# Latent attention with the values stationary and two heads in one product's columns, and filler pieces placed in other spots

## The chip, the cores and the metric

The kernel runs on one core of a Trainium2 chip. The metric is the device time of one execution in microseconds (us), median of the runs. The core has five engines that run side by side and wait for one another by semaphores: TensorE (PE in the rows; its weight loads are PEld), VectorE (DVE), ScalarE (ACT), GpSimd (POOL) and SyncE (SP, which only issues transfers here). Each engine works through its instructions in the order in which the program lists them.

## The reference, cut to what matters

A first block mixes four branches over 1024 tokens of width 1024, then a feed-forward part and a gate; a second block has linear attention of two kinds and 16 experts. The change touches the latent attention and the state-space branch (SSD) of the first block, the start of its feed-forward part, and the gated linear attention of the second block.

```python
def mla_mixer(c_q, c_kv, k_r, cos, sin, q_norm, w_uq, kv_norm, w_ukv):   # 8 heads, 64 + 32 wide
    ...
    for blk in range(s // Q_BLOCK):                                        # 8 blocks of 128 queries
        q0, kend = blk * Q_BLOCK, (blk + 1) * Q_BLOCK
        sc = (jnp.einsum('bqhd,bkhd->bhqk', q_nope[:, q0:kend], k_nope[:, :kend])
              + jnp.einsum('bqhd,bkd->bhqk', q_rope[:, q0:kend], k_rope[:, :kend]))
        ...
        sc = jnp.where(ki <= qi, sc, -jnp.inf)
        pr = jax.nn.softmax(sc, axis=-1).astype(v.dtype)
        outs.append(jnp.einsum('bhqk,bkhd->bqhd', pr, v[:, :kend]))

def ssd_mixer(z, xbc, dt, conv_w, conv_b, dt_bias, a_log, d_skip, norm_g): # 8 chunks of 128 tokens
    ...
    lmat = jnp.exp(segsum(a))
    cb = jnp.einsum('bclgn,bcsgn->bgcls', cm, bm)
    y_diag = jnp.einsum('bgrcls,bcsgrp->bclgrp', cb[:, :, None] * lmat, xdt)
```

## The kernel before, in words

All large products are made of three products each (helper `mm3`, lines 104 to 106): an operand is split into a high part and a low part (helper `split`, lines 94 and 96: ACT writes the high part, DVE the low one), and hi x hi, hi x lo and lo x hi are summed in PSUM. Their tiles are called `mm`. Operands of plain float32 are multiplied directly; the trace then has two weight loads and two matmuls for one product, called two passes here.

A queue of generators holds such work that nothing waits for at once: the `gates` products of the first block (16 weight chunks, 4 units each, a unit in three pieces of 9, 9 and 6 matmuls of 512 columns), then the first parts of the branch merge (`merge_ahead`, `merge_ahead0`), in the second block the `projections`. `fill(n)` takes n pieces from the queue and places them at that point of the program. The framework then orders the instructions of each engine by its own estimate, near the order of the program.

**SSD** (lines 409 to 480). For each of 8 chunks: `fill(6)`; transposes of the input (`s_tp`); `s_cb`; then for two groups g: POOL writes `s_al` (line 436), PE makes `s_sg` from it (line 440), ACT takes the exponential into `s_m` (line 442), DVE multiplies `s_m` by a mask (line 443), and PE makes `s_yd` of it (line 446, four heads of 64 columns); then `s_yo` and `s_ct` (lines 451, 456).

**Latent attention** (`mla`). Four head groups hg of two heads each. In each group: keys and values (`kv_tile`), queries (`q_tile`), turned by PE (`m_kt`, line 583); then 16 steps s = (i, h) over 8 query blocks i and 2 heads h. A step has the scores `sc` of 128 queries against n = 128(i+1) keys (line 604; PSUM tile `sc` exists once), the maximum on DVE (lines 607, 608), the exponential and its sum on ACT (line 611), the transposes of the weights by 128 columns (`m_pt`, line 629), copied to SBUF by DVE or ACT (`m_pT`, lines 632, 634), and the product with the values `m_o` (line 638): the weights' transpose is stationary (128 x 128), 64 columns of values `m_v` stream. DVE divides by the sum (`m_ot`, lines 640, 641). After both heads PE transposes the result (`m_yt`, line 644), ACT copies it and POOL issues its store. `scores` of the next step stand ahead of the transposes of this one, and `fill(1 + s % 2)` between transposes and `m_o`.

**Feed-forward start** (group g == 0): tokens 512 to 1023 are normed (`norm_half`), then eight products `ff1`. **Gated linear attention** (`gla`): four steps of `decays` (DVE and ACT) and `states` (transposes `g_ktp` line 1305, products `g_ct` line 1312), `fill(2)` between; then scores `g_s` (line 1361), where two heads use 64 rows of the array each.

## Time and profile before

| what | before |
|---|---|
| median of 3 runs | 3830.4 us (3830.1 to 3832.64) |
| profiled execution, its own time | 3829.97 us |
| its span, first to last instruction | 3828.3 us |
| PE busy | 3645.7 us, 95% of the span |
| DVE, ACT, POOL busy | 57%, 42%, 16% |
| mean granted clock of TensorE | 0.98 of full speed |

The profile is one execution recorded by the hardware. A busy PE is not PE at its peak, since matmuls are pipelined: how long a run of them really takes is read from the distance of the starts. A granted clock of 1.00 is the level of 2.4 GHz, and a mean below it says that a part of the stretch ran at 1.2 GHz.

### The profile page before, as it was taken

The page shows a single profiled execution, that of the slowest core. Times are in us where ns is not written, and L with a number is a line of the kernel's source. Part 1 is how long each engine was busy: PE and PEld are TensorE (multiplying, and loading weights), DVE is VectorE, ACT ScalarE, POOL GpSimd, SP SyncE. Part 2 cuts the span into 40 slices and gives each one's busy share as a digit, 9 for nine tenths or more (in the row PEclk, how much of TensorE's full clock was granted, in tenths as well). Part 3 has the DMA queues.
Part 4 walks back from the last instruction along what each step waited for, and adds up shares of the span by engine and source line. Part 5 has one row for each costly group of instructions (what it writes and reads, how often), then busy time and mean ns, then how long its engine had stood idle before and what let it go on. Part 6 is the DMA issues. An engine that isn't in the chain of part 4 may idle for free.

```text
span 3828.3 us, 50597 instructions
## 1 busy us (share of the span) xinstructions
PE 3645.7 (95%) x19648; PEld 3023.6 (79%) x19648; DVE 2184.7 (57%) x3304; ACT 1595.1 (42%) x2310; POOL 618.8 (16%) x731
## 2 busy tenths in 40 slices
PE   8999899999999899999999999989996999999997
PEld 6787688888779888888888988878985677777775
DVE  5425523333455566555435556575554688877777
ACT  7432243333333222222224656445242566654555
POOL 0002310101122200000000211222331222222111
PEclk9999999999999999999999999999997999999999
DMA  4211111221366423332213252223366799998987
GB/s 124 74 51 53 63 51 57 68 65 51 121 196 184 132 79 93 110 96 92 88 45 105 78 144 65 78 79 113 115 219 237 248 354 364 370 347 325 356 335 267
DMA packets 309037, 583.07 MB, mean 152 GB/s; under 512 B 27342, under 2 KB 211756, under 8 KB 308796
## 3 DMA queue, kind: packets, MB, share of 16 engines
q1 hardware_dynamic: 286508, 509.52, 39.0%
q0 software_dynamic: 22288, 70.31, 5.4%
q8 instruction: 155, 2.54, 0.3%
q14 instruction: 86, 0.70, 0.1%
HBM read 513.66 MB, written 66.09 MB: 151 GB/s over the span
## 4 chain that ended last, share of the span: by engine, by line
PE 68%; DVE 5%; issue 4%; ACT 3%; DMA 3%; POOL 2%; SPq 0%; DVEq 0%; POOLq 0%; ACTq 0%
PE mm L104 13%; PE mm L105 13%; PE mm L106 13%; PE mm L1831 5%; PE mm L1828 5%; PE mm L1829 5%; PE mm L1827 5%; PE sc L604 2%; PE m_o L638 1%; DMA w_raw<-in_w_in_dram 1%; DVE w_lo L96 1%; PE m_pt L629 1%; DMA m_g<-gates 1%; DVE e_lo L1804 1%; PE g_s L1361 1%
## 5 line engine op out<-in xcount | busy, mean ns | idle before, releaser
L104 PE MATMUL mm<-hh_hi,w_hi 128*128 128x512 f32 x1872 | 748.7, 400 | 5.4 <-ACT p_u L321 2.1
L105 PE MATMUL mm<-hh_lo,w_hi 128*128 128x512 f32 x1872 | 738.0, 394 | 0.1
L106 PE MATMUL mm<-hh_hi,w_lo 128*128 128x512 f32 x1872 | 737.1, 394 | 0.5 <-DVE w_lo L96 0.5
L1804 DVE TENSOR_TENSOR e_lo<-e_raw,e_hi 128x1408 fp32r<-128x1408 f32 (+1 forms) x308 | 502.5, 1671 | 59.2 <-ACT e_hi L1803 57.5
L96 DVE TENSOR_TENSOR w_lo<-w_raw,w_hi 128x1024 fp32r<-128x1024 f32 (+4 forms) x284 | 348.9, 1244 | 245.9 <-ACT w_hi L94 244.3
L1803 ACT ACTIVATE e_hi<-e_raw 128x1408 fp32r<-128x1408 f32 (+1 forms) x308 | 408.7, 1373 | 139.7 <-PE mm L1829 67.4
L104 PEld LDWEIGHTS mm<-hh_hi,w_hi 128*128 128x128 f32 x1872 | 354.0, 189 | 81.4 <-issue 5.1
L106 PEld LDWEIGHTS mm<-hh_hi,w_lo 128*128 128x128 f32 x1872 | 353.5, 189 | 77.6 <-issue 2.7
L105 PEld LDWEIGHTS mm<-hh_lo,w_hi 128*128 128x128 f32 x1872 | 354.3, 189 | 71.6 <-issue 3.3
L94 ACT ACTIVATE w_hi<-w_raw 128x1024 fp32r<-128x1024 f32 (+4 forms) x284 | 273.6, 985 | 326.8 <-PE mm L105 177.7
L104 PE MATMUL mm<-w_hi,hh_hi 128*128 128x256 f32 x1152 | 334.4, 291 | 0.0
L105 PE MATMUL mm<-w_lo,hh_hi 128*128 128x256 f32 x1152 | 328.5, 285 | 0.0
L106 PE MATMUL mm<-w_hi,hh_lo 128*128 128x256 f32 x1152 | 327.4, 285 | 0.0
L104 PEld LDWEIGHTS mm<-w_hi,hh_hi 128*128 128x128 f32 x1152 | 221.6, 193 | 4.1 <-issue 0.2
L105 PEld LDWEIGHTS mm<-w_lo,hh_hi 128*128 128x128 f32 x1152 | 222.0, 193 | 2.0 <-issue 1.5
L106 PEld LDWEIGHTS mm<-w_hi,hh_lo 128*128 128x128 f32 x1152 | 221.6, 193 | 0.1
L1827 PE MATMUL mm<-e_hi,e_xh 128*128 128x512 f32 x540 | 208.0, 409 | 0.0
L1828 PE MATMUL mm<-e_lo,e_xh 128*128 128x512 f32 x540 | 203.8, 377 | 0.0
L1829 PE MATMUL mm<-e_hi,e_xl 128*128 128x512 f32 x540 | 203.6, 377 | 0.0
L105 PE MATMUL mm<-w_lo,a_hi 128*128 128x512 f32 x512 | 199.6, 390 | 0.0
L104 PE MATMUL mm<-w_hi,a_hi 128*128 128x512 f32 x512 | 199.6, 390 | 0.0
L106 PE MATMUL mm<-w_hi,a_lo 128*128 128x512 f32 x512 | 199.3, 389 | 0.0
(653 smaller groups left out, 6625.4 us busy)
## 6 DMA issues: line engine op xcount, KB each, us to landing
e_raw<-in_w_exp_down_dram SPq DMA_DIRECT2D x112, 768.0 KB
e_raw<-in_w_exp_gate_dram SPq DMA_DIRECT2D x90, 704.0 KB
e_raw<-in_w_exp_up_dram SPq DMA_DIRECT2D x90, 704.0 KB
w_raw<-in_w_in_dram SPq DMA_DIRECT2D x82, 512.0 KB
w_raw<-in_w_ff_dram SPq DMA_DIRECT2D x64, 512.0 KB
w_raw<-in_w_ada_dram SPq DMA_DIRECT2D x48, 512.0 KB
e_nat<-in_w_exp_up_dram SPq DMA_DIRECT2D x32, 704.0 KB
e_nat<-in_w_exp_gate_dram SPq DMA_DIRECT2D x30, 704.0 KB
```

The costliest lines, as they stand in the source:

```text
L94: S.activation(hi, src, AF.Copy, scale=1.0 if scale is None else scale)
L96: V.tensor_sub(lo, src, hi.bitcast(F32))
L104: P.matmul(ps, ah, bh, start=start and k == 0, stop=False)
L105: P.matmul(ps, ah, bl, start=False, stop=False)
L106: P.matmul(ps, al, bh, start=False, stop=stop and k == nk - 1)
L604: P.matmul(sc[:, b:e], qT[:, h, i * 128:n], kT[:, h, b:e], start=True, stop=e < n)
L1803: S.activation(hi[:, :n], r[:, :n], AF.Copy)
L1804: V.tensor_sub(lo[:, :n], r[:, :n], hi[:, :n].bitcast(F32))
L1827: P.matmul(ps, x[0][:, k], w[0][:, c0:c1], start=k == 0, stop=False)
L1828: P.matmul(ps, x[0][:, k], w[1][:, c0:c1], start=False, stop=False)
L1829: P.matmul(ps, x[1][:, k], w[0][:, c0:c1], start=False, stop=k == last)
L1831: P.matmul(ps, x[2](k), w[:, c0:c1], start=k == 0, stop=k == last)
```

## The change

In SSD the six pieces of filler of a chunk stand in three places: one ahead of the chunk, three between the two groups' `s_sg`, two between the two groups' `s_yd`; both groups' `s_m` are started before the first `s_yd`. In the attention the weights are divided by their sum on DVE before they are transposed (n columns, not 64), the values become the stationary operand (128 x 64) and 128 columns of transposed weights stream; the two heads write to partitions 0 to 63 and 64 to 127 of the same `m_o` tile, so the result is feature-major and `m_yt` on PE and `m_ot` on DVE fall away. For i of 4 and more, the first 512 keys and the rest are two separate groups of products. Buffers: `m_pT` 2 to 3, `m_kx` 3 to 2, `m_yt` 2 to 1. The filler's amount in SSD and attention stays the same (6 pieces a chunk, 3 pieces a query block). In the feed-forward start the norm of each 128 tokens follows one product. In `gla` the first of four steps has `fill(4)`.

```diff
@@ -406,7 +406,7 @@
             ssq = sp.tile([128, NT], F32, name="s_ssq")
             B8 = lambda t: t[:, :, None].to_broadcast([128, 8, 64])
             for c in range(NT):
-                fill(6)
+                fill(1)
                 tk = slice(c * 128, (c + 1) * 128)
                 p = ps_ax("s_tp")
                 for ft in range(4):
@@ -430,8 +430,8 @@
                     P.transpose(p[:, :128], xT[:, 4, tk], ident)
                     bt = sp.tile([128, 128], F32, name="s_bt", bufs=2)
                     S.activation(bt, p[:, :128], AF.Copy)
-                yd = ps_ax("s_yd")
-                for g in range(2):
+                def segments(g):
+
                     al = sp.tile([128, 2, 4, 128], F32R, name="s_al4", tag="s_xin", bufs=2)
                     G.tensor_mul(al, triu[:, None, None, :].to_broadcast([128, 2, 4, 128]),
                                  a_p[:, :, c, g * 4:(g + 1) * 4, None].bitcast(F32).to_broadcast([128, 2, 4, 128]))
@@ -441,9 +441,18 @@
                     m = sp.tile([128, 4, 128], F32, name="s_m", bufs=2)
                     S.activation(m.rearrange("p a b -> p (a b)"), p, AF.Exp)
                     V.tensor_mul(m, m, cbm[:, g, None, :].to_broadcast([128, 4, 128]))
+                    return m
+
+                yd = ps_ax("s_yd")
+                ms = [segments(0)]
+                fill(3)
+                ms.append(segments(1))
+                for g in range(2):
+                    if g:
+                        fill(2)
                     for r in range(4):
                         h = g * 4 + r
-                        P.matmul(yd[:, h * 64:(h + 1) * 64], m[:, r], xdt[:, h], start=True, stop=True)
+                        P.matmul(yd[:, h * 64:(h + 1) * 64], ms[g][:, r], xdt[:, h], start=True, stop=True)
                 y = sp.tile([128, 8, 64], F32, name="s_y", bufs=2)
                 V.tensor_add(y, yd.rearrange("p (h q) -> p h q", q=64), xsk)
                 if c > 0:
@@ -562,7 +571,7 @@
                     p = ps_mm()
                     mm3(p[:, :256], cT, wkv, 2, lambda t, k: t[:, 3 + k, tk], lambda t, k: t[:, k, :])
                     p4 = p[:, :256].rearrange("p (h d) -> p h d", h=2)
-                    kx = mp2.tile([128, 2, 96], F32, name="m_kx", bufs=3)
+                    kx = mp2.tile([128, 2, 96], F32, name="m_kx", bufs=2)
                     V.tensor_scalar(kx[:, :, :64], p4[:, :, :64], rs[:, 1, i:i + 1], None, op0=OP.mult)
                     S.activation(vt[:, i], p4[:, :, 64:], AF.Copy, scale=rs[:, 1, i:i + 1])
                     G.tensor_copy(kx[:, :, 64:], krr[:, i:i + 1].to_broadcast([128, 2, 32]))
@@ -572,7 +581,7 @@
                     tk = slice(i * 128, (i + 1) * 128)
                     p = ps_mm()
                     mm3(p[:, :192], cT, wuq, 3, lambda t, k: t[:, k, tk], lambda t, k: t[:, k, :])
-                    q0 = mp2.tile([128, 2, 96], F32, name="m_kx", bufs=3)
+                    q0 = mp2.tile([128, 2, 96], F32, name="m_kx", bufs=2)
                     S.activation(q0.rearrange("p a b -> p (a b)"), p[:, :192], AF.Copy, scale=rs[:, 0, i:i + 1])
                     rope(q0[:, :, 64:], i, 2)
                     return q0
@@ -597,6 +606,7 @@
                         turn(dst, src, i)
 
                 def scores(i, h):
+
                     n = (i + 1) * 128
                     sc = ps_sc()
                     for b in range(0, n, 512):
@@ -609,44 +619,64 @@
                     pr = mp2.tile([128, T], F32, name="m_p", bufs=2)
                     rsum = mp2.tile([128, 1], F32, name="m_rsum", bufs=4)
                     S.activation(pr[:, :n], sc[:, :n], AF.Exp, scale=scale, bias=mx, accum_out=rsum)
-                    return pr, rsum
-
-                steps = [(i, h) for i in range(NT) for h in range(2)]
-                ahead = scores(*steps[0])
-                for s, (i, h) in enumerate(steps):
-                    pr, rsum = ahead
+                    V.reciprocal(rsum, rsum)
+                    V.tensor_scalar(pr[:, :n], pr[:, :n], rsum, None, op0=OP.mult)
+                    return pr
+
+                def turned(pr, h, b, e):
+
+                    pt = ps_ax("m_pt")
+                    for k in range(b, e, 128):
+                        P.transpose(pt[:, k - b:k - b + 128], pr[:, k:k + 128], ident)
+                    pT = mp2.tile([128, 512], F32, name="m_pT", bufs=3)
+                    if h == 0 or b == 0 and e < 512:
+                        V.tensor_copy(pT[:, :e - b], pt[:, :e - b])
+                    else:
+                        S.activation(pT[:, :e - b], pt[:, :e - b], AF.Copy)
+                    return pT
+
+                prs = [scores(0, 0), scores(0, 1)]
+                for i in range(NT):
                     n = (i + 1) * 128
-                    if h == 0:
-                        o = ps_mm("m_o")
-                        ot = mp2.tile([128, 2, 64], F32, name="m_ot", bufs=2)
-                    if s + 1 < len(steps):
-                        ahead = scores(*steps[s + 1])
-                    pTs = []
-                    for b in range(0, n, 512):
-                        e = min(n, b + 512)
-                        pt = ps_ax("m_pt")
+                    o = ps_mm("m_o")
+
+                    def attend(pTs, b, e):
+
                         for k in range(b, e, 128):
-                            P.transpose(pt[:, k - b:k - b + 128], pr[:, k:k + 128], ident)
-                        pT = mp2.tile([128, 512], F32, name="m_pT", bufs=2)
-                        if b == 0:
-                            V.tensor_copy(pT[:, :e - b], pt[:, :e - b])
-                        else:
-                            S.activation(pT[:, :e - b], pt[:, :e - b], AF.Copy)
-                        pTs.append(pT)
-                    fill(1 + s % 2)
-                    for k in range(0, n, 128):
-                        P.matmul(o[:, h * 64:(h + 1) * 64], pTs[k // 512][:, k % 512:k % 512 + 128], vt[:, k // 128, h],
-                                 start=k == 0, stop=k // 128 == i)
-                    V.reciprocal(rsum, rsum)
-                    V.tensor_scalar(ot[:, h], o[:, h * 64:(h + 1) * 64], rsum, None, op0=OP.mult)
-                    if h == 1:
-                        pt = ps_ax("m_yt")
-                        P.transpose(pt[:, :128], ot.rearrange("p h d -> p (h d)"), ident)
-                        yt = mp2.tile([128, 128], F32, name="m_yt", bufs=2)
-                        S.activation(yt, pt[:, :128], AF.Copy)
-                        G.dma_start(Yd[0][hg * 128:(hg + 1) * 128, i * 128:n], yt)
-                        if hg == 3 and i == 3:
-                            queue.append(merge_ahead0())
+                            for h in range(2):
+                                P.matmul(o[h * 64:(h + 1) * 64, :128], vt[:, k // 128, h], pTs[h][:, k - b:k - b + 128],
+                                         start=k == 0, stop=k // 128 == i)
+
+                    nx = [None, None]
+                    def more(h):
+                        if i + 1 < NT:
+                            nx[h] = scores(i + 1, h)
+
+                    if n <= 512:
+                        t0 = turned(prs[0], 0, 0, n)
+                        more(0)
+                        fill(1)
+                        t1 = turned(prs[1], 1, 0, n)
+                        more(1)
+                        fill(2)
+                        attend((t0, t1), 0, n)
+                    else:
+                        t0 = turned(prs[0], 0, 0, 512)
+                        t1 = turned(prs[1], 1, 0, 512)
+                        u0 = turned(prs[0], 0, 512, n)
+                        more(0)
+                        fill(1)
+                        attend((t0, t1), 0, 512)
+                        u1 = turned(prs[1], 1, 512, n)
+                        more(1)
+                        fill(2)
+                        attend((u0, u1), 512, n)
+                    prs = nx
+                    yt = mp2.tile([128, 128], F32, name="m_yt", bufs=1)
+                    S.activation(yt, o[:, :128], AF.Copy)
+                    G.dma_start(Yd[0][hg * 128:(hg + 1) * 128, i * 128:n], yt)
+                    if hg == 3 and i == 3:
+                        queue.append(merge_ahead0())
 
 
     def sincos(sn, cs, ang, pool):
@@ -857,10 +887,11 @@
             wf1 = lambda q: fetch(w_ff1[:, :, g * 512 + q * 128:g * 512 + q * 128 + 256], KD, 256)
             if g == 0:
                 w = [wf1(0), wf1(2)]
-                norm_half(1, g_mlp, range(4, 8))
-                for h in range(2):
-                    for q in range(4):
-                        act[q, h] = ff1(w[q // 2], q, h)
+                for q in range(4):
+                    act[q, 0] = ff1(w[q // 2], q, 0)
+                    norm_half(1, g_mlp, [4 + q])
+                for q in range(4):
+                    act[q, 1] = ff1(w[q // 2], q, 1)
                 fill(1)
             else:
                 for q in range(4):
@@ -1327,7 +1358,7 @@
             la = decays(*steps[0])
             for s, (d, h) in enumerate(steps):
                 nla = decays(*steps[s + 1]) if s < 3 else None
-                fill(2)
+                fill(4 if s == 0 else 2)
                 states(d, h, la)
                 la = nla
             for h in range(2):
```

Three places of PE's order show what moves. The first is the third SSD chunk. Before, all products `s_tp` to `s_ct` stand together with six filler matmuls among them ("..." is 5 filler matmuls; 42 more stand behind `s_ct`):

```order
L413 MATMUL s_tp<-ident,s_x 128x128 x4
L426 MATMUL s_cb<-s_x 128x128 x2
L440 MATMUL s_sg<-s_al_2554,s_sgr 128x512 x2
L440 MATMUL s_sg<-s_al_2566,s_sgr 128x512 x2
L104 MATMUL mm<-hh_hi,w_hi 128x512
L430 MATMUL s_bt<-ident,s_x 128x128
...
L446 MATMUL s_yd<-s_xdt,s_m 128x64 x8
L451 MATMUL s_yo<-s_st_2222,s_x 128x512
L456 MATMUL s_ct<-s_xdd,s_bt 128x512
```

In the changed kernel the same chunk reads as follows ("..." leaves out 3 filler matmuls ahead of `s_bt`, 20 between it and the second `s_sg`, 15 between the two `s_yd`; 9 follow `s_ct`):

```order
L413 MATMUL s_tp<-ident,s_x 128x128 x4
L426 MATMUL s_cb<-s_x 128x128 x2
L440 MATMUL s_sg<-s_al_2508,s_sgr 128x512 x2
L104 MATMUL mm<-hh_hi,w_hi 128x512
...
L430 MATMUL s_bt<-ident,s_x 128x128
...
L440 MATMUL s_sg<-s_al_2544,s_sgr 128x512 x2
L455 MATMUL s_yd<-s_xdt,s_m 128x64 x4
...
L455 MATMUL s_yd<-s_xdt,s_m 128x64 x4
L460 MATMUL s_yo<-s_st_2222,s_x 128x512
L465 MATMUL s_ct<-s_xdd,s_bt 128x512
```

The filler moved from behind the chunk to the places between a group's `s_sg` and its `s_yd`. The second to fourth and the sixth to eighth chunk read much like this; in the first and the fifth there are 5 and 2 filler matmuls, not 20, between the last `s_cb` and the first `s_yd`.

The second place is the attention of the first head group, from the scores of i = 7 on. Before (an x7 of `m_o` or `m_pt` is seven products; "..." is the mask's product `m_neg` and, ahead of `m_o`, 17 filler matmuls):

```order
L604 MATMUL sc<-m_kT,m_qT 128x512 x2
...
L629 MATMUL m_pt<-ident,m_p 128x128 x7
...
L638 MATMUL m_o<-m_v,m_pT 128x64 x7
L604 MATMUL sc<-m_kT,m_qT 128x512
L644 MATMUL m_yt<-ident,m_ot 128x128
L604 MATMUL sc<-m_kT,m_qT 128x512
...
L629 MATMUL m_pt<-ident,m_p 128x128 x8
```

In the changed kernel ("..." is 6, 2 and 16 filler matmuls, the first and the last with the mask's product):

```order
L614 MATMUL sc<-m_kT,m_qT 128x512 x2
...
L647 MATMUL m_o<-m_pT,m_v 64x128 x8
L630 MATMUL m_pt<-ident,m_p 128x128 x3
...
L614 MATMUL sc<-m_kT,m_qT 128x512 x2
...
L647 MATMUL m_o<-m_pT,m_v 64x128 x6
L630 MATMUL m_pt<-ident,m_p 128x128 x12
```

The products with the values stand in 12 groups in each head group, 4 to 16 products a group, the two heads in turn; `m_yt` is gone.

The third place is the first `states` step of `gla` for the second pair of heads. Before ("..." is 47 and 4 filler matmuls), with the next step's transposes right behind:

```order
L1282 MATMUL g_pre<-g_z,g_w 128x512 x2
...
L1305 MATMUL g_ktp<-ident,g_la 128x128 x4
...
L1312 MATMUL g_ct<-g_v,ho_y 128x256 x4
L1282 MATMUL g_pre<-g_z,g_w 128x512
L1305 MATMUL g_ktp<-ident,g_la 128x128 x4
```

In the changed kernel ("..." is 47, 4 and 12):

```order
L1313 MATMUL g_pre<-g_z,g_w 128x512 x2
...
L1336 MATMUL g_ktp<-ident,g_la 128x128 x4
...
L1343 MATMUL g_ct<-g_v,ho_y 128x256 x4
L1313 MATMUL g_pre<-g_z,g_w 128x512
...
L1336 MATMUL g_ktp<-ident,g_la 128x128 x4
```

Here the added filler stands ahead of the second `g_ktp`, and none was added ahead of the first.

## Rows read from the trace of the kernel before

**Rows 1.** The page, part 1: engine, busy us (share of span), instructions.
```profile
PE 3645.7 (95%) x19648; PEld 3023.6 (79%) x19648; DVE 2184.7 (57%) x3304; ACT 1595.1 (42%) x2310; POOL 618.8 (16%) x731
```

**Rows 2.** Stretches: length, busy PE, PEld, DVE, ACT, POOL; clock, DMA share, GB/s.
```profile
322.00:484.00 162.00, 141.77 (x651) 108.56 (x649) 86.56 (x110) 40.31 (x73) 55.89 (x48) 0.95 0.17 54
...
598.00:683.00 85.00, 84.76 (x478) 68.29 (x476) 30.71 (x81) 24.82 (x57) 8.32 (x16) 1.00 0.14 47
...
995.00:1105.00 110.00, 102.57 (x524) 79.71 (x523) 68.51 (x122) 42.38 (x77) 22.10 (x22) 0.94 0.50 149
```

**Rows 3.** Waits of PE in 322 to 484: us, times, longest.
```profile
PE s_yd L446 <- DVE s_m L443: 19.8, 10, 3.6
```

**Rows 4.** Timeline of an SSD chunk: start, duration, engine, line.
```profile
387.96 4.61 POOL L436 TENSOR_TENSOR s_al<-triu,s_ap 128x1024 fp32r<-128x1024 f32 x2
388.43 4.68 DVE L443 TENSOR_TENSOR s_m<-s_m,s_cbm 128x512 f32<-128x512 f32 x2
...
390.87 1.10 PE L446 MATMUL s_yd<-s_xdt,s_m 128*128 128x64 f32 x8 [1.08 <-DVE s_m L443]
```

**Rows 5.** Line 443: durations in ns, minimum, median, maximum.
```profile
L443 DVE TENSOR_TENSOR s_m<-s_m,s_cbm x16: 678/2379/4817, 324.7 to 474.5; 128x512 f32<-128x512 f32 x16
```

**Rows 6.** Timeline of PE, attention's fourth group: filler and score passes of 128 columns.
```profile
862.46 0.39 PE L604 MATMUL sc<-m_kT,m_qT 96*128 96x128 f32 x2
...
862.68 0.22 PE L605 MATMUL sc<-m_neg,identb 128*128 128x128 bf16 x1
...
863.26 0.40 PE L106 MATMUL mm<-hh_hi,w_lo 128*128 128x512 f32 x1
...
863.49 0.40 PE L104 MATMUL mm<-hh_hi,w_hi 128*128 128x512 f32 x1
```

**Rows 7.** Timeline of PE at the attention's end.
```profile
1094.68 1.89 PE L638 MATMUL m_o<-m_v,m_pT 128*128 128x64 f32 x16
1096.40 1.05 PE L629 MATMUL m_pt<-ident,m_p 128*128 128x128 f32 x8
1099.04 2.00 PE L638 MATMUL m_o<-m_v,m_pT 128*128 128x64 f32 x16 [1.59 <-DVE m_pT L632]
1101.42 0.33 PE L644 MATMUL m_yt<-ident,m_ot 128*128 128x128 f32 x1 [0.38 <-DVE m_ot L641]
```

**Rows 8.** Tiles m_o and m_yt: instructions and durations in ns.
```profile
L638 PE MATMUL m_o<-m_v,m_pT x576: 217/275/323, 598.8 to 1100.8; 128*128 128x64 f32 x192
L644 PE MATMUL m_yt<-ident,m_ot x32: 271/275/473, 604.5 to 1101.4; 128*128 128x128 f32 x32
```

**Rows 9.** Timeline of PE, gla's scores: 16 passes, two sets of 64 rows.
```profile
2450.91 0.28 PE L106 MATMUL mm<-w_hi,hh_lo 128*128 128x256 f32 x1
2451.12 1.16 PE L1361 MATMUL g_s<-g_X 64*128 64x128 f32 x16
...
2452.21 0.39 PE L104 MATMUL mm<-w_hi,hh_hi 128*128 128x256 f32 x1
```

**Rows 10.** Groups by shape, 598 to 1105: busy us, mean ns, idle before.
```profile
L607 DVE TENSOR_REDUCE m_mx<-sc 128x1 f32<-128x1024 f32 x8 | 9.8, 1223 | 9.8 <-PE sc L605 9.8
...
L611 ACT ACTIVATE m_p<-sc,m_mx 128x1024 f32<-128x1024 f32 x8 | 8.9, 1115 | 3.9 <-DVE m_mx L608 3.9
```

**Rows 11.** Line 393: a DVE scaling of 1024 columns in SBUF.
```profile
L393 DVE TENSOR_SCALAR s_x<-s_xin,par x6: 748/752/755, 257.6 to 313.3; 128x1024 f32<-128x1024 f32 x6
```

**Rows 12.** Stretches at the fourth group's hole and end, and the feed-forward start.
```profile
1005.00:1015.00 10.00, 6.12 (x25) 3.65 (x24) 7.76 (x15) 6.58 (x12) 1.33 (x3) 0.73 0.67 214
...
1095.00:1105.00 10.00, 7.66 (x47) 6.52 (x46) 5.83 (x8) 3.17 (x5) 1.83 (x2) 0.84 0.47 138
...
1360.00:1400.00 40.00, 40.00 (x182) 32.75 (x181) 18.72 (x34) 11.74 (x18) 1.16 (x2) 1.00 0.20 66
```

**Rows 13.** Timeline of PE in gla's second pair, first states step.
```profile
2503.86 1.12 PE L1305 MATMUL g_ktp<-ident,g_la 128*128 128x128 f32 x4 [5.25 <-DVE g_la L1299]
...
2534.67 1.35 PE L1312 MATMUL g_ct<-g_v,ho_y 128*128 128x256 f32 x4 [1.94 <-ACT ho_y L1307]
```

## The prediction

> **What bounds the kernel now.** I read the page first, then the stretches of the stages that the diff touches, then in each stage what PE waits for, and last the distances of starts of the instructions that change. The page says that PE is the bound: busy 95% of the span, DVE 57% [rows 1]. But the share is an average, so each stage is judged alone. SSD lies between 322 and 484 us: PE works 141.77 of 162 us there, so 20.2 us are idle, and the mean clock is 0.95 [rows 2]. Nearly all of that idle time has one cause: PE waits for `s_m` ahead of `s_yd`, 19.8 us in ten waits [rows 3]. One chunk shows how: all of a chunk's products are queued first, six filler matmuls follow, and then PE stands before both halves of `s_yd` while DVE needs 4.68 us for the two products `s_m`, exactly while POOL writes two `s_al` in 4.61 us [rows 4]. Alone such a product takes 0.68 us, with POOL beside it 2.4 or more [rows 5]. In the attention it is the other way round: the first head group keeps PE busy for 84.76 of 85 us at full clock [rows 2], so nothing can be gained there but PE's own time. Only the fourth group has a hole (7.4 us idle in 110, clock 0.94) [rows 2].
>
> **SSD: filler moved, none added.** Six pieces a chunk stay six. In the changed order 24 matmuls stand between the first `s_sg` and the first `s_yd`, beside the second `s_sg`, and 15 between the two halves. A filler matmul is 0.23 us from start to start [rows 6], so the covers are 5.5 us and 3.45 us. Needed are the exponential of 512 columns (about 0.6 us, half of what 1024 take in [rows 10]) and one product `s_m` of 0.68 to 2.4 us [rows 5], with hand-overs some 3.4 us. Both are covered in six of eight chunks; one weight split of DVE in between (about 1.2 us for 1024 columns, the size of the maximum in [rows 10]) may still show. In the first and fifth chunk the cover is 5 and 2 matmuls, and I leave 2 us a chunk there. I take 5 us of the 20.2 as left, so 15 are won. The clock: 0.05 of 162 us is 8.1 us lost to the lower level, partly while PE stood still anyway; with gaps gone I take 5 back. Together **-20 us**; bounds -10 (every second wait stays, the clock half) and -28 (all). What was hidden behind the filler at the chunk's start, the next `s_tp`, loses cover from 42 matmuls to 9: DVE must have released a PSUM bank and finished the chunk's sums within 2.1 us, which is as long as its two or three products of 0.7 us; that is in the 5 us left.
>
> **Attention: the product with the values.** Now 576 passes [rows 8], bound by loading 128 stationary columns: 16 of them take 1.72 us, from 1094.68 to 1096.40, 0.1075 each [rows 7], 61.9 us in all, though only 64 columns stream. With the values stationary, half as many columns are loaded, but 128 plain float32 columns stream, and a pass that streams 128 takes 0.11 us too (two score passes from 862.46 to 862.68) [rows 6]. So one pass after another the swap wins nothing: all hangs on the two heads running side by side in the two halves of the array's columns. The trace before has no such product. Its nearest row is `g_s`, where two heads use two halves of the array's rows: 16 passes of 128 streamed columns in 1.09 us up to the next matmul's start, 0.068 each [rows 9], where 16 one by one would be 1.76. Ahead of them the distance is 0.21 us, some 0.1 more than a matmul of 256 columns needs (half of 0.23). So a group of p passes costs (p/2 + 1) x 0.11 + 0.2 us: 1.19 for 16, as measured. The order has 12 groups in each of four head groups, 48 with 576 passes: 288 x 0.11 + 48 x 0.31 = 46.6 us. The 32 transposes `m_yt` [rows 8] go too, 0.11 each, 3.5 us. Saved: 61.9 + 3.5 - 46.6 = 18.8 us.
>
> The Trainium skill (TensorE: Matmul & The Clock Gate, "Part 3: Packing small matmuls") says that products in different column groups run together as those in different row groups do; no run here shows it for columns. By it the sum is the one above; by the row of one pass after another [rows 6] the change would cost: 576 x 0.11 + 48 x 0.2 - 65.4 = +7.6 us. Against the change stands its page TensorEngine Tiling (Array Packing), "Key Properties": a change of tiling mode drains the engine. Trace: 0.1 us at an end in [rows 9]. If a drain were a matmul's whole length (0.275 us [rows 8] less 0.11, so 0.17 at each of 96 ends), 6.7 us less would be saved. I keep 0.1, since it is measured at the nearest product.
>
> **Attention: what the order now exposes.** DVE's division of 64 columns becomes one of n columns, 0.75 us for 1024 [rows 11]; DVE is busy 30.71 of 85 us there [rows 2], so its time is hidden, and the scaled weights are needed only 16 matmuls and a group later (over 4 us). More delicate: `sc` exists once, so the second head's scores wait for the first head's maximum and exponential, 1.22 + 1.12 us at 1024 keys [rows 10], with hand-overs and the small scaling some 2.9. Before, 17 fillers, 7 transposes and 14 passes lay between, 6.2 us. Now it is 6 and 2 fillers (1.84), a group of 16 (1.19) and 3 transposes (0.33): 3.4 us. That suffices unless ACT or DVE has a filler's piece in front, a gate's exponent or a weight split of 0.6 to 1.2 us; then PE stalls about half a microsecond. For one in eight of 64 that is 4 us; bounds 0 and 15. So **-15 us** for the attention, bounds -28 (free switches, no stall) and +8.
>
> **The rest.** The fourth group's hole (3.9 us idle from 1005 to 1015 [rows 12]) lies where the gates' filler has ended and the merge's weights and branches are being loaded (DMA share 0.67 there [rows 12], 0.14 in the first group [rows 2]); it is as long as the transfers and does not shrink. At the attention's end `m_yt` and its wait go (0.38 us) and the last wait for a copy shortens from 1.59 us [rows 7]: -1 us. `gla`: the 5.25 us wait ahead of the first `g_ktp` [rows 13] keeps its 47 fillers and stays; the added filler helps a later spot, waits there are below 2 us [rows 13]: -1.5, bounds 0 and -3. The feed-forward start: PE is busy for 40 of 40 us from 1360 to 1400 [rows 12], so there is nothing to win; the norms' DVE and ACT work is hidden behind the products either way; uncovered, each of the four would cost at least a pass over 1024 columns on DVE, 0.75 to 1.2 us by [rows 10, 11]: 0. Buffers: `m_kx` with two is turned by PE before the next but one is written in this order; `m_yt` with one waits for a store that has a whole query block's time: 0.
>
> **Sum.** -20 - 15 - 1 - 1.5 = -37.5 us from the profiled execution's 3829.97 us, 3792.5; the median of the runs is 0.4 higher: **3793 us**. 0.2%, about what a measurement of this kernel tells from no change, is 7.7 us.
>
> **The rivals.**
> (A) As summed: 3778 to 3808 us, 3793. Chance 0.62.
> (B) The column halves take turns. For it: no row shows columns side by side. Against: the rows' halves do [rows 9]. -20 - 2.5 + 7.6: 3815 us. Chance 0.16.
> (C) SSD keeps its waits: `s_al` of the next chunk is written right behind each `s_sg`, so DVE's product again runs beside POOL, up to 4.8 us [rows 5], and every second half is exposed. SSD then gives 6 us and not 20: 3807 us. Chance 0.10.
> (D) Slower: the single `sc` becomes the attention's clock. If the second scores wait 1 us at each of 64 score products, because DVE's new scaling and the fillers' splits stand ahead of the maximum, that costs 64 us against 41 won elsewhere: 3853 us. It decides from 0.65 us a product. Against: the cover of 3.4 us is longer than the chain of 2.9 even at 1024 keys, and the chain shrinks with n. Chance 0.06.
> (E) B and C together, no change that can be told: -6 - 2.5 + 7.6, 3829 us. Chance 0.06.
>
> **Range.** A, B and C together hold 0.88 and lie from 3778 to 3815; with the bounds of the unknown costs 3770 to 3820. Faster by over 0.2%: 0.87; within: 0.07; slower: 0.06.
>
> **What would show it.** In the changed profile `m_o` must have 576 passes of 128 streamed columns, starting in pairs, a group of 16 in about 1.2 us (A) or 1.96 (B). Stretches of the four head groups' query blocks should each be about 4 us shorter, with PE still without idle time; idle time ahead of `sc` put down to ACT's exponential speaks for D. SSD should last some 142 us with 5 idle and the clock near 1.00; waits of `s_yd` for `s_m` of over 10 us speak for C. `g_ktp` should still wait about 5 us once in `gla`. I am wrong if the time won lies elsewhere, for instance in the merge, which the diff leaves alone, or if the shorter attention only lengthens the hole of the fourth group.

## The result and the profile after

The changed kernel takes 3788.8 us (median of four runs, 3785.6 to 3794.4) where the kernel before takes 3831.5 beside it: a ratio of 0.9889, 95% interval 0.9872 to 0.9906, so 1.1% faster. The profiled execution has a span of 3783.9 us, 44.4 less than before. Its page begins so (part 1, busy time and share of the span):

```profile
span 3783.9 us, 50508 instructions
## 1 busy us (share of the span) xinstructions
PE 3618.3 (96%) x19616; PEld 2978.2 (79%) x19616; DVE 2186.6 (58%) x3300; ACT 1609.2 (43%) x2321; POOL 627.9 (17%) x731
```

PE is still the bound, as in [rows 1]. Three stretches of the changed kernel, with the columns of [rows 2] (length, busy PE, PEld, DVE, ACT, POOL; clock, DMA share, GB/s): SSD, the first head group's query blocks, and the hole of the fourth group.

```profile
311.50:459.70 148.20, 143.37 (x704) 111.61 (x703) 83.95 (x121) 49.98 (x81) 61.02 (x51) 1.00 0.22 70
...
570.00:654.50 84.50, 84.50 (x492) 61.25 (x491) 36.39 (x85) 27.59 (x64) 8.87 (x17) 1.00 0.15 49
...
966.00:976.00 10.00, 5.61 (x20) 2.74 (x18) 7.81 (x15) 6.17 (x10) 0.54 (x1) 0.75 0.64 204
```

SSD stands still for 4.8 us and not 20.2, at full clock. The window is not 142 us long, as the prediction's sign has it, but 148.2: only one piece of filler stands ahead of the first chunk now and not six, so the window takes in 53 matmuls more and the stretch before it is shorter (101.3 and not 110.2 us, below). The hole in the third row is the one of [rows 12], neither longer nor shorter by more than a microsecond. What PE waits for in SSD now (us in total, times, longest), against the one row of [rows 3]:

```profile
PE s_yt L486 <- DVE s_z L482: 2.1, 2, 1.2
PE s_yd L455 <- DVE s_m L443: 1.3, 1, 1.3
PE s_bt L430 <- DVE s_xsk L419: 1.0, 2, 0.5
PE s_yd L455 <- DVE s_cbm L427: 0.4, 1, 0.4
```

The wait for `s_m` has gone from ten times to one, in the first chunk. A chunk's timeline shows why, beside [rows 4]: the first half of `s_yd` runs, DVE then has its second product for 1.87 us, beside POOL's next `s_al`, and PE reaches the second half with no idle time named, since two pieces of filler stand between.

```profile
370.66 0.39 PE L440 MATMUL s_sg<-s_al,s_sgr 128*128 128x512 f32 x1
370.89 1.00 PE L455 MATMUL s_yd<-s_xdt,s_m 128*128 128x64 f32 x8
...
371.21 1.89 POOL L436 TENSOR_TENSOR s_al<-triu,s_ap 128x1024 fp32r<-128x1024 f32 x1 [1.12 <-PE s_sg L440]
...
371.78 1.87 DVE L443 TENSOR_TENSOR s_m<-s_m,s_cbm 128x512 f32<-128x512 f32 x1 [5.37 <-ACT s_m L442]
...
375.21 1.00 PE L455 MATMUL s_yd<-s_xdt,s_m 128*128 128x64 f32 x8
```

In the attention `m_o` has as many passes as in [rows 8], now of 128 streamed columns on 64 output columns; the first fence is its row among the instructions of PE (busy us, mean ns, idle before), the second a group of 16 in the timeline of PE.

```profile
L647 PE MATMUL m_o<-m_pT,m_v 128*64 128x128 f32 x576 | 42.9, 283 | 0.4 <-ACT m_pT L635 0.4
```

```profile
650.06 0.39 PE L105 MATMUL mm<-hh_lo,w_hi 128*128 128x512 f32 x1
650.29 0.39 PE L106 MATMUL mm<-hh_hi,w_lo 128*128 128x512 f32 x1
650.61 1.09 PE L647 MATMUL m_o<-m_pT,m_v 128*64 128x128 f32 x16
651.63 0.39 PE L104 MATMUL mm<-w_hi,m_chi 128*128 128x256 f32 x1
```

The group takes 1.02 us to the next start, where 16 passes before took 1.72 [rows 7]: the first pass starts 0.09 late (0.32 after the filler and not 0.23), and groups of 8, 12 and 16 take 0.59, 0.81 and 1.02, so a further pass costs about 0.0535 us. The starts come in pairs 0.007 us apart, one pass of each head, as the prediction's sign asked. In `gla` the wait of [rows 13] has grown instead:

```profile
2461.60 1.12 PE L1336 MATMUL g_ktp<-ident,g_la 128*128 128x128 f32 x4 [7.14 <-DVE g_la L1330]
```

Going by the starts on PE, the time won is in two places. The first `m_ssp` starts 26.3 us earlier, the first `m_hi` behind the attention 46.1; from there on it moves between 36 and 46, and the last matmul starts 45.2 earlier. The stretch from the first `m_hi` to the first `c_st`, which almost no edit touches, varies from 1151 to 1157 us over all the kernels below: differences of that size in one profile say nothing by themselves.

### The profile page after: what moved, and what is told of

Read it like the earlier page. It is cut to its first block, busy times and chain, and to the rows that moved or that the text cites. A ratio compares the mean times of both kernels' runs of the same rounds, so it can differ in the third digit from the quotient of the medians.

```text
span 3783.9 us, 50508 instructions
## 1 busy us (share of the span) xinstructions
PE 3618.3 (96%) x19616; PEld 2978.2 (79%) x19616; DVE 2186.6 (58%) x3300; ACT 1609.2 (43%) x2321; POOL 627.9 (17%) x731
## 4 chain that ended last, share of the span: by engine, by line
PE 65%; DVE 6%; issue 5%; DMA 4%; ACT 3%; POOL 3%; SPq 0%; DVEq 0%; POOLq 0%; ACTq 0%
PE mm L104 13%; PE mm L106 13%; PE mm L105 13%; PE mm L1862 5%; PE mm L1859 5%; PE mm L1860 5%; PE mm L1858 5%; DMA m_g<-gates 2%; PE sc L614 1%; DVE w_lo L96 1%; PE m_o L647 1%; PE m_pt L630 1%; POOL m_acc L771 1%; DVE e_lo L1835 1%; PE e_at L1993 1%
```

## The experiments

Diffs are against the changed kernel, unless said otherwise. Times are medians, beside the kernel before on the same chip.

**SSD's edits alone** (in the kernel before).

> The kernel before with the change's edits in SSD alone (filler spread over the chunk, both segments first). Theory: SSD is worth the 25 to 26 us by which m_ssp starts earlier in the changed kernel, and the rest of the program passes that on: 3831.5 - 25.5 = about 3806 us (3803 to 3809), SSD about 148 us long at clock 1.00, attention as before with head groups of about 89.2 us up to the next m_kt. Rival: SSD gives the 20 us of the prediction and part of the 25 belongs to the attention's edits, through the filler that they share: 3811 us or more.

Measured: 3798.5 us beside 3828.2, ratio 0.9928 (0.9914 to 0.9941), 28 us by the ratio (23 to 33). The first `m_ssp` starts 25.3 us earlier than in the kernel before, and the waits and the stretch of SSD are those of the changed kernel:

```profile
312.90:461.10 148.20, 143.33 (x704) 111.62 (x703) 83.52 (x121) 49.56 (x81) 61.42 (x52) 1.00 0.22 70
```

So SSD gives 25 us and needs the attention's edits for none of it. The time is below the expected 3803 to 3809, in part because the kernel before was 3.3 us faster beside it; the 2 to 3 us over 25 can't be told from noise.

**The attention's edits alone** (in the kernel before, with the buffers).

> The kernel before with the change's edits in the attention alone (and its buffers). Theory: four head groups shorter by 4.5 us each and the end by under 1 us, independent of SSD: 3831.5 - 18.5 = 3813 us (3810 to 3816); m_o in groups of 16 that take about 1.0 us. Rival: without the 25 us won in SSD the filler stands elsewhere, the single sc shows waits and the gain is under 12 us: 3820 us or more.

Measured: 3810.8 us beside 3828.2, ratio 0.9954 (0.9940 to 0.9967), 17.6 us by the ratio. A group of 16 takes the same time as in the changed kernel. Both halves together give 1.18%, the whole change 1.1 to 1.2%: they add up, and the rival falls.

**The same products, heads in turn.**

```
-                        for k in range(b, e, 128):
-                            for h in range(2):
+                        for h in range(2):
+                            for k in range(b, e, 128):
                                 P.matmul(o[h * 64:(h + 1) * 64, :128], ...
```

> The changed kernel, but in each group all products of the first head, then all of the second, so that neighbours on PE use the same half of the columns; number, shapes and results of the products are the same. Theory (the two halves of the columns run side by side, and only neighbours in different halves do): a pass goes back from 0.0535 to about 0.11 us, 576 x 0.056 = 32 us slower, 3821 us (3815 to 3825); a group of 16 takes about 1.9 us. Rival (the halved weight load of 64 columns is what became faster): a group of 16 stays at about 1.0 us and the time at 3789 us within 4.

Measured: 3799.6 us beside 3828.2, ratio 0.9929 (0.9914 to 0.9944); the changed kernel on that measure is 3785 us, so 14 us slower and neither 32 nor 0. A group of 16 in the timeline of PE:

```profile
634.79 0.40 PE L106 MATMUL mm<-hh_hi,w_lo 128*128 128x512 f32 x1
635.12 1.58 PE L647 MATMUL m_o<-m_pT,m_v 128*64 128x128 f32 x16
636.63 0.55 PE L630 MATMUL m_pt<-ident,m_p 128*128 128x128 f32 x3
```

It takes 1.51 us, a group of 12 takes 1.08, but a group of 8 (four passes of each head) still 0.59 as in the alternating order. A group of 4 says nothing here: it has one product of two passes for each head, and the edit leaves its order as it was. So the order of heads matters, as the theory says, but the second head's passes do not wait until the first head's are done: in the group of 16, starts some 0.11 us apart come singly from 635.12 on, at 635.61 a second such row sets in beside the fifth start of the first, and the last four starts come singly again. Twelve steps of 0.109 and 0.2 us are the 1.51. A head group has six groups of 16 and two of 12: 6 x 0.49 + 2 x 0.27 = 3.5 us, 14 us in four, which is the time measured. My number was wrong because I took the halves to work together only between neighbours.

**Both heads in one half**, which takes the other half away altogether.

```
+                    def attend_low(pTs):
+                        for h in range(2):
+                            for k in range(0, n, 128):
+                                P.matmul(o[:64, h * 128:(h + 1) * 128], vt[:, k // 128, h], pTs[h][:, k:k + 128],
+                                         start=k == 0, stop=k // 128 == i)
                     if n <= 512:
...
-                        attend((t0, t1), 0, n)
+                        attend_low((t0, t1))
```

> The changed kernel, but in query blocks 0 to 3 both heads' products go to the lower half of the columns, one head after the other (two stores per block instead of one, buffers of the maxima 3 instead of 4); blocks 4 to 7 as in the changed kernel. With the heads in turn but in different halves, groups of 4, 8, 12 and 16 passes took 0.37, 0.59, 1.08 and 1.51 us. Theory (each half of the columns runs its own passes at 0.107 us and some four passes can run ahead in the other half): in one half nothing overlaps, the groups take 0.107 each and 0.1 to 0.2 for the change of form, about 0.5, 1.0, 1.4 and 1.85 us; the time about 9 us over the changed kernel. Rival (a product of 64 output columns is quicker by itself, in whichever half, and the order of heads costs for another reason): 16 passes in 1.0 to 1.5 us.

Measured in one run: 3796.7 us, where the changed kernel has 3784.0 on that chip. Its group of 16:

```profile
605.57 0.39 PE L106 MATMUL mm<-hh_hi,w_lo 128*128 128x512 f32 x1
605.89 1.96 PE L654 MATMUL m_o<-m_pT,m_v 128*64 128x128 f32 x16
607.78 1.20 PE L630 MATMUL m_pt<-ident,m_p 128*128 128x128 f32 x9
```

Groups of 4, 8, 12 and 16 take 0.58, 1.02, 1.46 and 1.89 us, where the same head order in two halves took 0.37, 0.59, 1.08 and 1.51. The step is now 0.11 us a pass. The product of 64 output columns is not quicker by itself; the two halves working side by side are the gain. The groups make 2.2 us in each of the first three head groups, about 9 in four as expected; the rest of the 12.7 lies in the fourth group, and it is a single run. One half with the two heads alternating was not run. That successive sums into one place are what costs 0.11 is unlikely, since the transposes `m_pt`, each into a place of its own, start 0.109 us apart too.

**SSD's filler back at the chunk's start.**

```
-                fill(1)
+                fill(6)
...
                 ms = [segments(0)]
-                fill(3)
                 ms.append(segments(1))
                 for g in range(2):
-                    if g:
-                        fill(2)
```

> The changed kernel, but SSD's six pieces of filler stand at the start of a chunk again, as before, while both segments are still computed ahead of both halves of s_yd. Theory (the place of the filler is the gain): PE waits for s_m again, once a chunk about 2 to 3 us, SSD some 16 to 22 us longer, 3805 to 3811 us. Rival (starting both segments early is the gain, POOL being out of DVE's way): SSD stays within 5 us of the changed kernel's 148, 3789 to 3794 us.

Measured: 3814.7 us beside 3828.2, ratio 0.9968 (0.9957 to 0.9979), some 29 us over the changed kernel. The wait of [rows 3] and the stretch of [rows 2] are back, almost to the digit:

```profile
PE s_yd L452 <- DVE s_m L443: 19.9, 10, 3.6
```

```profile
321.00:483.20 162.20, 141.93 (x645) 108.45 (x644) 86.58 (x110) 38.80 (x71) 55.45 (x47) 0.94 0.17 54
```

All of SSD's gain is the filler's place; computing both segments first gives nothing by itself. The expected price was too small: from the first `s_cs` to the first `m_ssp` this kernel takes 321.3 us where the changed one takes 294.4, and the part over the idle time, about 10 us, is the lower clock.

**SSD's segments one by one**, the filler at its new places.

```
                 ms = [segments(0)]
-                fill(3)
-                ms.append(segments(1))
                 for g in range(2):
                     if g:
-                        fill(2)
+                        ms.append(segments(1))
+                    fill(2 if g else 3)
```

> The changed kernel, but SSD's second segment is issued only behind the first half of s_yd; the filler keeps its new places, three pieces behind the first s_sg and two behind the second. Theory (the filler right behind the products that are waited for is the whole gain): each half still has 3 to 5 us of cover, so at most 0.5 us a chunk is lost, 0 to 4 us over the changed kernel. Rival (both segments must be under way early): the second half shows a wait of 2 us or more in most chunks, 12 to 20 us slower.

Measured: 3788.3 us beside 3831.5, ratio 0.9891 (0.9870 to 0.9911). SSD's stretch keeps 143.35 busy of 148.20 us and its waits are those of the changed kernel to 0.1 us. This is the other half of the same proof: the second segment need not be early, the filler must stand right behind the products that are waited for.

**The weights scaled twice.**

```
                     V.tensor_scalar(pr[:, :n], pr[:, :n], rsum, None, op0=OP.mult)
+                    V.tensor_scalar(pr[:, :n], pr[:, :n], 1.0, None, op0=OP.mult)
```

> The changed kernel, but DVE multiplies each tile of weights a second time, by 1.0: 64 more passes over 128 to 1024 columns, about 27 us of DVE's time in all. Theory (the scaling lies beside PE's work, and the one buffer of scores has enough filler before it): 0 to 3 us over the changed kernel, PE still without idle time in the first three head groups. Rival (DVE's new pass is on the way to the next scores, the prediction's case D): 10 to 27 us slower, as idle time of PE ahead of sc and m_pt.

Measured: 3787.9 us beside 3831.5, ratio 0.9889 (0.9868 to 0.9910), as the changed kernel. The first head group shows DVE at 43.44 us and not 36.39, and PE with 0.09 us of idle time:

```profile
570.00:654.50 84.50, 84.41 (x492) 61.13 (x491) 43.44 (x101) 27.27 (x64) 9.59 (x17) 1.00 0.15 51
```

So even twice the scaling is hidden in the first three head groups, and the prediction's case D was far off.

**The changed kernel again, and without its last edits.** The second kernel has `fill(2)` at every step of `gla`; the third has that and the feed-forward's start of before.

> The changed kernel itself once more, as the measure for the next ones on the same chip. Every theory: 0.989 of the kernel before, about 3786 us if that takes 3828 us.

> The changed kernel, but with two pieces of filler ahead of every step of gla, as before. Theory: the added filler harms, because its copies and weight splits stand before the decays on DVE and ACT: PE's longest wait of g_ktp for g_la is 5.2 to 5.5 us again and not 7.1 to 7.5, and the distance from c_st to q_t, which grew by 1.7 us in the changed kernel and shrank by 3.3 and 4.2 us in the two half changes without this edit, shrinks by 3 to 4: about 5 us faster than the changed kernel. Rival (the prediction's term): the filler helps a later wait, so 1.5 us slower than the changed kernel.

> The changed kernel without its last two edits: gla's filler and the order of norms and products at the feed-forward's start are those of before. Theory: the feed-forward's order gives nothing (PE was busy there for 40 of 40 us either way), so within 2 us of the kernel with gla's edit alone undone. Rival: norms between the products hide something that they cost before: 2 to 5 us slower than that kernel.

Measured beside 3830.5: 3784.0 (ratio 0.9879, 0.9862 to 0.9895), 3782.4 (0.9874, 0.9857 to 0.9890) and 3782.1 us (0.9876, 0.9860 to 0.9893). In the time the three can't be told apart: the 5 us expected of `gla` are not there, though a loss below that is not excluded. The feed-forward's order gives 0.3 us, that is nothing, as expected. In the profiles the longest wait of `g_ktp` is 7.4 us with the edit and 6.0 and 5.3 without.

**`gla`'s edit alone**, in the kernel before.

```
-                fill(2)
+                fill(4 if s == 0 else 2)
                 states(d, h, la)
```

> The kernel before with gla's edit alone (four pieces of filler instead of two ahead of the first of four steps). In the profiles so far, from the first c_st to the first r_kt seven kernels with the edit took 371.6 to 377.1 us and six without it 362.8 to 369.9; from there to the first q_t the former took 141.7 to 144.0 and the latter 147.7 to 150.1. Theory: the edit itself does this: about 375 and 143 us, longest wait of g_ktp 7 us or more, 2 to 5 us slower than before in the stretch and 0 to 5 us in the time, up to 3835 us if the kernel before takes 3830. Rival (the shift of the filler comes from the earlier edits, or the prediction's term of 1.5 us won holds): 366 and 150 us as before, or a time 1.5 us below it.

Measured: ratio 1.0010 (0.9998 to 1.0022) over twelve runs, no change that can be told. The profile shows the shift that was expected: 375.4 us from the first `c_st` to the first `r_kt` (366.0 before), 142.8 from there to the first `q_t` (149.8 before), 2.4 us more in sum. The longest wait of `g_ktp` is 6.1 us, below the 7 expected:

```profile
PE g_ktp L1305 <- DVE g_la L1299: 10.6, 3, 6.1
```

Over all profiles the sum of the two stretches is 513.4 to 520.3 us in eight kernels with the edit (mean 517.8) and 511.6 to 517.6 in six without (mean 513.9). The longest wait of `g_ktp` is 6.1 to 7.5 us in all eight and 5.2 to 6.0 in all six. So the edit brings filler forward from the retention into `gla`, lengthens that wait, and seems to lose some 4 us on the way. The size is not settled: the two sets overlap, the changed kernel alone gave 517.6 and 520.3 in two profiles (513.7 with this edit undone), and the kernel before 515.8 without and 518.2 with the edit. In the times the interval of the last pair goes from 0.8 us won to 8.4 lost, which leaves out the 1.5 us won of the prediction, by little.

**The hole moved**, in the kernel without the last two edits.

```
     def merge_ahead():
         y2[:] = [half(), half()]
         y_load(0, (1, 3, 2))
-        yield
+        for _ in range(5):
+            yield
...
-    fill(4)
+    fill(24)
     mla()
```

> The changed kernel without gla's and the feed-forward's edits, with 24 pieces of filler instead of 4 between SSD and the latent attention, and four pieces without work behind the load of the merge's branches: the gates' filler ends sooner, so that the load falls into the projections of the fourth head group, where PE has work of its own, and not into its first query blocks. Theory: the fourth group's hole (4.7 us idle and the clock at 0.80 and 0.69 in two stretches of 10 us) closes, 1 to 3 us of short waits come in the projections: 3 to 5 us faster than the kernel with the two edits undone, about 3778 us if the kernel before takes 3830. Rival (the prediction's view, the hole is as long as the transfers wherever it lies): the same within 2 us.

Measured: 3801.5 us beside 3831.5, ratio 0.9925 (0.9910 to 0.9941), some 18 us slower than without it: both theories fall. Two stretches, the fourth group's projections, into which the load now falls, and its query blocks:

```profile
915.00:960.00 45.00, 43.03 (x278) 33.69 (x277) 22.72 (x36) 21.85 (x44) 8.79 (x15) 1.00 0.42 128
...
1000.00:1030.00 30.00, 23.99 (x88) 13.82 (x89) 11.78 (x33) 6.88 (x19) 1.62 (x3) 0.64 0.15 44
```

The load itself was hidden well (2 us idle in 45). But the filler is a fixed stock: 20 pieces, 44 us of PE's work, spent ahead of the attention are missing from the fourth group's query blocks, which have 60 filler matmuls and not 222. In the 30 us of the second row PE stands still for 6 us and the clock falls to 0.64; over all these blocks it is idle for 13.5 us at a clock of 0.79, where the kernel without the move has 8.2 us and 0.97, and these two differences together make up about the 18 us. Moved in this way the hole cost more than it gave; another way was not tried. No version tried is measurably faster than the changed kernel.

## Why the prediction was right, point by point

The forecast was 3793 us, case A; the time is 3788.8, inside A's own bounds. Both large terms were too small, by 8 us together, and one small one probably had the wrong sign, so the total is nearer than its parts: that much is luck.

**SSD, -20 forecast, -25 measured.** The mechanism is as predicted: the wait for `s_m` is covered by moved filler. The 5 us left over came out as 4.8, but mostly elsewhere: the first and the fifth chunk, for which the forecast left 2 us each, wait 1.3 and 0.4 us, and 3.1 us are waits for `s_z` and `s_xsk`. The next `s_tp`, which it feared for, never waits. From the first `s_cs` to the first `m_ssp` the kernel before takes 319.5 us and the changed one 294.4; idle time falls from 21.0 to 4.8, and PE's busy time from 298.5 to 289.6. These are the windows of both, the kernel before first, split at the first `s_tp`:

```profile
211.80:322.00 110.20, 110.20 (x620) 97.05 (x621) 39.15 (x35) 32.45 (x49) 4.77 (x7) 1.00 0.18 51
322.00:531.30 209.30, 188.26 (x861) 146.44 (x860) 102.91 (x169) 56.18 (x97) 64.19 (x72) 0.96 0.15 50
```

```profile
210.60:311.90 101.30, 101.30 (x580) 89.69 (x581) 33.31 (x30) 30.26 (x47) 2.31 (x5) 1.00 0.15 42
311.90:505.00 193.10, 188.27 (x900) 148.45 (x899) 97.22 (x175) 63.75 (x104) 68.74 (x74) 1.00 0.19 61
```

The 8.9 us less of busy time, for 1480 matmuls where there were 1481, are the clock: "with gaps gone I take 5 back" is the step that was mis-sized. It put part of the lower clock on time in which PE stood still anyway. In the trace none of it lies there: in the second row before, the clock is at 1.2 GHz five times, 17.1 us together, each time shortly after a wait for `s_m` of 1.2 to 3.6 us, when PE was at work again. Here is one of the five, then the eight passes of `s_yd` in it, 1.56 us to the next start, and the eight of a chunk of the changed kernel, 0.81 us:

```profile
330.45:333.85 3.40, 3.40 (x13) 2.69 (x12) 1.59 (x4) 0.00 (x0) 0.00 (x0) 0.50 0.00 0
```

```profile
331.26 1.80 PE L446 MATMUL s_yd<-s_xdt,s_m 128*128 128x64 f32 x8
332.82 0.77 PE L105 MATMUL mm<-hh_lo,w_hi 128*128 128x512 f32 x1
```

```profile
336.85 1.00 PE L455 MATMUL s_yd<-s_xdt,s_m 128*128 128x64 f32 x8
337.66 0.48 PE L104 MATMUL mm<-hh_hi,w_hi 128*128 128x512 f32 x1
```

In sum the starts in the five stretches are 8.8 us further apart than the same pairs of instructions at 2.4 GHz, so the whole loss came back. Case C, that every second wait stays, is excluded by the one wait left: DVE's product does run beside POOL again, as C has it, but 1.87 us of it lie behind the filler.

**The product with the values, -18.8 forecast, -18 measured.** The sum (p/2 + 1) x 0.11 + 0.2 a group held, though in other parts: a pass costs 0.0535 us, and adding up the distances of starts in the first head group `m_o` falls from 15.1 to 9.7 us and `m_yt` from 0.9 to 0, while the filler before gets 0.8 and the transposes `m_pt` 1.3 us longer. That is 4.5 us for the group, where the formula gives 4.7. The page of the Trainium skill on TensorE (TensorE: Matmul & The Clock Gate, "Part 3: Packing small matmuls") says that column groups run together, and these traces agree: 0.0535 us a pass in two halves, 0.11 in one. The Trainium skill (TensorEngine Tiling (Array Packing), "Key Properties") says that a change of tiling mode drains the engine; what these traces show there is 0.09 us ahead of a group and about as much behind it. The price of a whole matmul's length that I had weighed against it did not come. Case B falls.

**New stalls, +4 forecast, 0 measured.** This is the other term that was off: "for one in eight of 64 that is 4 us". The single `sc` shows no wait in the first three head groups, and even with DVE's scaling doubled the first has 0.09 us idle. The cover of 3.4 us against a chain of 2.9 was right: at 1024 keys, from the end of the first head's scores, the second's start 3.3 to 3.5 us later and the exponential that they wait for ends 2.7 to 3.1 us later. A filler's piece in front of ACT or DVE that breaks this, the reason for the 4 us, does not show. Only in the fourth group, without filler, does PE wait for ACT's exponential: 5.6 us in five waits, 1.0 in two before, where it waited 5.4 us for `m_ot`, `m_pT` and `m_mx` instead. That is case D's wait, in the one place where no filler covers it.

**The attention's end, -1 forecast.** The two waits of 1.59 and 0.38 us [rows 7] and one of 0.37 behind them, for the copy `m_yt`, are now two of 0.37 and 0.70: -1.3.

**`gla`, -1.5 forecast, some +4 in the mean of the profiles, no change that can be told in the times.** The step that failed is "the added filler helps a later spot". No help shows: the 47 fillers ahead of the first `g_ktp` stay, as I had read, but its wait grows from 5.25 to 7.14 us, and the filler that is spent here is missing later. That its weight splits and copies on DVE and ACT delay the decays is argued from the row, not shown.

**Feed-forward and buffers, 0 forecast.** The feed-forward's order undone changes nothing; PE was busy all along there. The buffers were never tried by themselves, but from 570 to 912 us PE waits 0.5 us in all, and not for `m_kx`.

**The fourth group's hole, no change forecast.** It stayed, and moving it cost 18 us.

## What to carry to other kernels

Look for the wait behind a stage's products before adding work to hide it: here the same six pieces of filler cost 25 us at the wrong place, two thirds of it idle time and one third the clock that fell behind it. When a product has few output columns, give its neighbours different halves of the array's columns and alternate them; the price is a change of form of about a tenth of a microsecond at either end of a group, so groups of four passes no longer win (0.37 us and 0.09 ahead of it, where two groups of two took 0.17 each before). Filler is a stock: whoever spends it earlier must look at the stage that had it last.

## What the hardware did that I had not expected

- Passes for two column halves need not alternate strictly. With all of one head's passes first, four and then four took the same 0.59 us as in the alternating order; six and six lost 0.27 and eight and eight 0.49 us, about two and four steps of 0.109. So, by these times and the spacing of the starts, four passes of the second head ran beside the last four of the first in each of these groups, ahead of passes that the program lists before them.
- SSD with gaps also varies more from one execution to the next. From the first `s_tp` to the first `m_ssp` the four kernels with the filler at the chunk's start took 209.3 to 215.9 us, three of them with the very same code there; the nine with the filler spread and nothing else moved took 193.0 to 193.2 us each time. The gaps do not vary, the clock does: the four are idle for 20.7 to 21.1 us, and their mean granted clock there is 0.96, 0.94, 0.92 and 0.95 for 209.3, 212.0, 215.9 and 211.1 us.
